# Key pages of a paged cache loaded two to a tile: one layer of a hybrid attention trunk on one core

## The chip, the cores and the metric

The kernel runs on one core of a Trainium2 chip. The core has a matrix engine (PE), whose weight loads are shown as PEld, a vector engine (DVE), an activation engine (ACT), a general engine (POOL), a queue engine (SP) and 16 DMA engines. The metric is the device time of one execution in microseconds (us). All arithmetic is float32; products that must be exact to float32 are made from a rounded high part and a low part (fp32r), so one product is three matmuls, or two where one side is used as it is.

## The reference

One layer serves a prompt of 1024 tokens and a sample group of 8 sequences with one new token each. A single input projection gives the queries, keys and values of a sparse attention (compressed blocks, selected blocks, sliding window), the input of a pooling mixer, the queries of an attention into 256 memory tokens, and gates. The three branches are gated, merged, projected and added, and a SwiGLU follows. For the sample group the past keys stand in a paged cache:

```python
past = nsa_pool_l[page_table].reshape(b, -1, 4, KV_HEADS, HEAD_DIM)
full = jnp.concatenate([past, nsa_kv], axis=1)
o_cmp, o_sel = nsa_cmp_sel(q, pos, full[:, :, 0], full[:, :, 1], full[:, :, 2], full[:, :, 3], l, w)
```

Every sequence has 16 pages of 128 tokens, 128 pages in all. Of each page the kernel needs the raw compression keys and values, summed over blocks of 32 tokens, and the scores of all selection keys against the new token's queries.

## The kernel before

All work stands in one function, `body`, and is written in stages: projections of prompt and sample together, memory attention and pooling mixer of the prompt, the sample group ("decode"), prompt attention in 32 units, merges, output projection, feed-forward. A planner at build time lists each engine's instructions in a fixed order; an engine then runs its list in that order and waits where an operand is late. The planner goes by priority, mostly the order of the program, and by when it thinks that buffers come free. Two kinds of work have low priority and fill PE's list wherever something else is late: the gate projections (`gates`, 24 tiles of 72 matmuls at L257) and the merges (`merge1f`, six tiles). A gate chunk collects in the PSUM bank `g` or `p`, one bank each, and ACT copies it out (`mg<-ps_g`, `mg<-ps_p`, L543); a bank takes the next chunk only after that copy.

SBUF tiles come from rings, in which a new tile takes a place that is free: the big ring T (12 tiles of 128x1032, `TT`), the small ring U (10 tiles of 128x512, `TU`), X (6 tiles of 128x512 for high and low parts, `TX`). T also holds what lives long in decode: the spread queries `qm` and `qmm`, the sums `pool2`, the scores `Ss`.

The stage that the change touches starts at L757. For each of 4 groups and 8 sequences, SP issues four page loads (`pages`, L724), each 128x384 into a U tile `kpg`: two times 128 columns of raw keys and values, 128 columns of selection keys. ACT rounds the selection keys to the high part `kph` (L239), POOL takes the difference `kpl` (L240), DVE sums the raw columns by blocks (L765, into `pool2`), and PE multiplies the high and low parts of the four pages with the spread queries (L768). After each group a `fold` (L729, L730) takes the scores out. Then the window keys follow (`wkt`, loaded at L778, stored again at L780, split, multiplied at L784) and the memory keys (`cmk`, loaded at L791), all in U tiles; then the selection by top-k, the value pages, and the prompt attention. In the attention, L1032 makes scores, L519 (DVE) and L522 (ACT) the softmax, L1043 to L1046 its sums, L1051 (POOL) scales, L1077 transposes, L239 and L240 split, and L1061 multiplies with the values. Merges use L1209 to L1223.

Of the kernel before, what the change touches and what calls it, by code (L numbers as in the profile page):

```python
# [10 lines left out]
ALU = mybir.AluOpType  # L11
AX = mybir.AxisListType
# [15 lines left out]
NPG = 16  # L28
# [165 lines left out]
def body(nc, tc, xT, memT, w_p, w_m, w_v, w_mk, w_mv, w_up, w_un, w_out, w_gu, w_dn, w_pool, w_cmp, gains, consts, jlt,  # L194
# [43 lines left out]
    def split(src, hi, lo, he=None, le=None):  # L238
        (he or S.copy)(hi, src)  # L239
        (le or V.tensor_sub)(lo, src, f(hi))  # L240
# [66 lines left out]
    def TU(name):  # L307
        return st_["tp"].tile([128, 512], F32, name=name, tag="U", bufs=NU)
# [101 lines left out]
    for j in range(4):  # L410
        q = proj(2 + j)
        hnorm(q, blk64, 1 / 64, gv("q"), split_sq=True)
        for s in range(2):
            h = 2 * j + s
# [301 lines left out]
    def pages(src, tab, jobs):  # L716

        p0 = jobs[0][1]
        with tc.issue_after(hist[-9].ins) if len(hist) >= 9 else nullcontext():
            rs = nc.values_load_multi_w_load_instructions(  # L720
                tab[0:1, p0:p0 + len(jobs)], engines=[mybir.EngineType.SP], min_val=0, max_val=PHYS - 1,
                skip_runtime_bounds_check_because="the table is clamped to the pages there are")[1]
        for (dst, _), r in zip(jobs, rs):
            hist.append(SY.dma_start(dst.rearrange("p (o c) -> p o c", o=1),  # L724
                                     src[bass.ds(r, 1)].rearrange("n p c -> p n c")))
# [30 lines left out]
    for g in range(4):  # L756
        ps = psum("s")  # L757
        for b in range(NB):
            h, l = TX("kph"), TX("kpl")
            kps = [TU("kpg")[:, :384] for _ in range(4)]  # L760
            pages(pgk, pts, [(kps[j], b * NPG + g * 4 + j) for j in range(4)])
            for j, kp in enumerate(kps):
                c = slice(j * 128, j * 128 + 128)
                split(kp[:, 256:], h[:, c], l[:, c], le=G.tensor_sub)
                V.tensor_reduce(pk3[:, :, b, g * 16 + j * 4:g * 16 + j * 4 + 4],  # L765
                                kp[:, :256].rearrange("p (s c l) -> p s c l", s=2, l=32), axis=AX.X, op=ALU.add)
            for x, kk in enumerate((h, l)):
                PE.matmul(ps, lhsT=qm[:, b * 128:b * 128 + 128], rhs=kk, start=b == 0 and x == 0,  # L768
                          stop=b == 7 and x == 1)
        fold(ps, Ss[(g // 2) * 64:(g // 2) * 64 + 64, (g % 2) * 512:(g % 2) * 512 + 512], 64, 512)  # L770
# [736 lines left out]
```

## Time and profile before

| | us |
|---|---|
| median of three runs | 1864.68 (1863.04 to 1869.71) |
| the profiled execution | 1865.09 |
| its span | 1863.3 |
| PE busy in the span | 1791.1 |
| DVE, ACT, POOL busy | 1210.4, 871.3, 738.1 |
| page stage: first to last page cast on ACT | 331.4 to 435.9 |
| prompt attention: first and last score matmul | 601.0 to 970.3 |

The span is the part of the execution that the trace covers. A busy time counts the instructions of an engine, not its waits; matmuls are pipelined, so the pace of a row of matmuls is read from their starts. An idle time is put down to the instruction that ended it.

### The profile page before, as it was taken

How to read it: one execution, taken by the hardware profiler on the slowest of the kernel's cores; microseconds unless marked ns; L12 is line 12 of the kernel's file. 1: busy time of each engine (PE TensorE's matmuls, PEld its weight loads, DVE VectorE, ACT ScalarE, POOL GpSimd, SP SyncE). 2: the span in 40 equal slices, each digit the busy share in tenths (PEclk: the TensorE clock that was granted, in tenths of full speed). 3: DMA queues.
4: the chain of work that ended last, by engine and by line, in shares of the span. 5: the costliest groups of instructions: out<-in, count | busy, mean ns of one | idle time of the engine just before them, and what ended most of it. 6: DMA issues, size and time to landing. Idle time of an engine off the chain costs nothing.

```text
span 1863.3 us, 34498 instructions
## 1 busy us (share of the span) xinstructions
PE 1791.1 (96%) x12337; PEld 1726.2 (93%) x12337; DVE 1210.4 (65%) x2748; ACT 871.3 (47%) x2012; POOL 738.1 (40%) x865
## 2 busy tenths in 40 slices
PE   6999999989999999989998999999999999999999
PEld 6998998888988999989998898999999999999999
DVE  8875788653555766788886835867666666635332
ACT  5743766444454766677764545423332332314100
POOL 5300211556342545467763337555455555100000
PEclk9999999899999999999999999999999999999999
DMA  4244124899665111452326643122222222546222
GB/s 169 100 142 141 63 101 164 303 303 317 202 211 169 52 47 63 140 193 90 94 84 195 196 135 95 65 85 80 70 84 80 80 86 77 170 126 183 59 68 94
DMA packets 142366, 241.13 MB, mean 129 GB/s; under 512 B 21449, under 2 KB 100450, under 8 KB 142194
## 3 DMA queue, kind: packets, MB, share of 16 engines
q1 hardware_dynamic: 118722, 189.69, 31.7%
q0 software_dynamic: 8496, 30.23, 5.0%
q10 hardware_dynamic: 14976, 19.01, 2.9%
q8 instruction: 97, 1.59, 0.4%
q14 instruction: 75, 0.61, 0.1%
HBM read 176.31 MB, written 62.55 MB: 128 GB/s over the span
## 4 chain that ended last, share of the span: by engine, by line
PE 53%; DMA 5%; DVE 4%; issue 2%; ACT 1%; POOL 1%; SPq 0%; DVEq 0%; POOLq 0%; ACTq 0%
PE ps_s L1391 10%; PE ps_t L1391 10%; PE ps_t L257 9%; PE ps_g L257 7%; PE ps_s L257 6%; PE ps_p L1061 3%; PE ps_s L1032 3%; PE ps_t L1077 2%; DMA mg<-acd 2%; PE ps_g L1391 2%; PE ps_p L1391 2%; DMA mg<-gd 1%; DMA olr<-od 1%; DMA x1d<-x 1%; DMA ad<-mg 1%
## 5 line engine op out<-in xcount | busy, mean ns | idle before, releaser
L257 PE MATMUL ps_g<-xh,wh 128*128 128x344 f32 x624 | 205.1, 329 | 4.3 <-ACT mg L543 3.9
L257 PE MATMUL ps_g<-xl,wh 128*128 128x344 f32 x624 | 201.4, 323 | 0.0
L257 PE MATMUL ps_g<-xh,wl 128*128 128x344 f32 x624 | 201.0, 322 | 0.0
L239 ACT CAST wh<-wr 128x512 fp32r<-128x512 f32 (+3 forms) x138 | 99.8, 746 | 185.4 <-PE ps_t L257 83.3
L1051 POOL TENSOR_SCALAR P<-P,st,gate 128x384 f32<-128x384 f32 (+2 forms) x192 | 127.9, 675 | 82.2 <-DVE st L1046 32.8
L239 ACT CAST cw<-tS 128x512 fp32r<-128x512 f32 x88 | 54.2, 619 | 183.9 <-PE ps_t L1391 99.4
L240 DVE TENSOR_TENSOR wl<-wr,wh 128x512 fp32r<-128x512 f32 (+3 forms) x112 | 103.7, 934 | 49.3 <-ACT wh L239 47.9
L257 PEld LDWEIGHTS ps_g<-xh,wh 128*128 128x128 f32 x624 | 118.1, 189 | 8.8 <-ACT mg L543 5.7
L522 ACT ACTIVATE P<-P,st 128x384 f32<-128x384 f32 (+2 forms) x192 | 112.2, 586 | 23.2 <-DVE st L519 21.2
L257 PEld LDWEIGHTS ps_g<-xl,wh 128*128 128x128 f32 x624 | 118.3, 190 | 1.6 <-issue 0.4
L257 PEld LDWEIGHTS ps_g<-xh,wl 128*128 128x128 f32 x624 | 118.0, 189 | 1.0 <-issue 0.2
L240 DVE TENSOR_TENSOR ptl<-ps_t,pth 128x512 fp32r<-128x512 f32 (+1 forms) x208 | 107.9, 529 | 15.6 <-ACT pth L239 14.1
L239 ACT CAST pth<-ps_t 128x512 fp32r<-128x512 f32 (+1 forms) x208 | 92.1, 457 | 52.9 <-PE ps_t L1077 37.4
L240 DVE TENSOR_TENSOR cw<-tS,cw 128x512 fp32r<-128x512 f32 x88 | 92.4, 1051 | 33.4 <-ACT cw L239 27.8
L1391 PE MATMUL ps_t<-t,cw 128*128 128x258 f32 x792 | 106.5, 283 | 2.4 <-DVE t L240 2.4
L1391 PE MATMUL ps_s<-t,cw 128*128 128x258 f32 x792 | 105.6, 282 | 2.7 <-ACT rq L274 2.7
L1391 PE MATMUL ps_s<-b,cw 128*128 128x258 f32 x792 | 107.4, 285 | 0.3 <-ACT p L1406 0.3
L1391 PE MATMUL ps_t<-b,cw 128*128 128x258 f32 x792 | 105.6, 282 | 0.3 <-issue 0.3
L1391 PEld LDWEIGHTS ps_s<-t,cw 128*128 128x128 f32 x792 | 99.5, 189 | 2.9 <-ACT rq L274 2.9
L1391 PEld LDWEIGHTS ps_t<-t,cw 128*128 128x128 f32 x792 | 99.4, 189 | 3.0 <-DVE t L240 3.0
L1391 PEld LDWEIGHTS ps_s<-b,cw 128*128 128x128 f32 x792 | 100.9, 191 | 0.7 <-ACT p L1406 0.5
L1391 PEld LDWEIGHTS ps_t<-b,cw 128*128 128x128 f32 x792 | 99.2, 188 | 0.7 <-issue 0.6
(527 smaller groups left out, 5642.0 us busy)
## 6 DMA issues: line engine op xcount, KB each, us to landing
kpg<-pg_k SPq DMA_DIRECT2D x128, 192.0 KB, 4.3
wr<-w_gu SPq DMA_DIRECT2D x44, 512.0 KB, 3.5
gd<-mg ACTq DMA_DIRECT2D x72, 172.0 KB, 3.4
wr<-w_m POOLq DMA_DIRECT2D x24, 512.0 KB, 5.5
acd<-zu SPq DMA_DIRECT2D x44, 258.0 KB, 2.1
mg<-acd SPq DMA_DIRECT2D x66, 172.0 KB, 3.2
mg<-gd SPq DMA_DIRECT2D x48, 172.0 KB, 2.4
wr<-w_p SPq DMA_DIRECT2D x16, 512.0 KB, 3.2
```

The costliest lines, as they stand in the source:

```text
L239: (he or S.copy)(hi, src)
L240: (le or V.tensor_sub)(lo, src, f(hi))
L257: PE.matmul(ps, lhsT=x, rhs=y, start=i == 0, stop=i == n - 1)
L522: S.activation(P[u], P[u], AF.Exp, bias=nm, scale=-1.0, accum_out=st[:, 6 + u:7 + u])
L1032: PE.matmul(ps, lhsT=u["q"][:, i * 128:i * 128 + 128], rhs=kk[:, k0 * 128 + a:k0 * 128 + a + n], start=x == 0, stop=x == 1)
L1051: lastp[:] = [G.tensor_scalar(p_, p_, st4[:, j, 5:6], gate[:, q, c:c + 1], op0=ALU.mult, op1=ALU.mult)]
L1061: PE.matmul(pv[:, c0:c0 + n], lhsT=lh, rhs=rhs, start=pvs["n"] == 0, stop=last, skip_group_check=True)
L1077: PE.transpose(pt_[:, x * 128:x * 128 + 128], pd[y][:, o - offs[y]:o - offs[y] + 128], ident)
L1391: PE.matmul(ps[c], lhsT=a[:, x * 512 + k * 128:x * 512 + k * 128 + 128], rhs=b[k][:, y * HT + c * HC:y * HT + c * HC + HC], start=first an ...
```

## The change

Two pages share one tile of the big ring, and the tiles of the small ring are no longer used for pages. Each page is still loaded by a DMA of its own. One ACT cast and one POOL difference round the selection keys of both pages (128x256 instead of 128x128), and the sums by blocks are made by two DVE instructions for two pages, one for keys and one for values, instead of one for each page. All lines behind it move down by three.

```diff
-            kps = [TU("kpg")[:, :384] for _ in range(4)]
-            pages(pgk, pts, [(kps[j], b * NPG + g * 4 + j) for j in range(4)])
+            kps = [TT(name="kpg")[:, :768].rearrange("p (j c) -> p j c", j=2) for _ in range(2)]
+            pages(pgk, pts, [(kps[j // 2][:, j % 2, :], b * NPG + g * 4 + j) for j in range(4)])
             for j, kp in enumerate(kps):
-                c = slice(j * 128, j * 128 + 128)
-                split(kp[:, 256:], h[:, c], l[:, c], le=G.tensor_sub)
-                V.tensor_reduce(pk3[:, :, b, g * 16 + j * 4:g * 16 + j * 4 + 4],
-                                kp[:, :256].rearrange("p (s c l) -> p s c l", s=2, l=32), axis=AX.X, op=ALU.add)
+                two_ = lambda t: t[:, j * 256:j * 256 + 256].rearrange("p (j c) -> p j c", j=2)
+                split(kp[:, :, 256:], two_(h), two_(l), le=G.tensor_sub)
+                for s in range(2):
+                    o = g * 16 + j * 8
+                    V.tensor_reduce(pk3[:, s, b, o:o + 8].rearrange("p (j c) -> p j c", j=2),
+                                    kp[:, :, s * 128:s * 128 + 128].rearrange("p j (c l) -> p j c l", l=32),
+                                    axis=AX.X, op=ALU.add)
```

Since the planner works with free places, the lists of all engines change from the page stage to the end of the merges. On SP, at the end of the page loads, the list before has the window loads (`wkt`), their stores (`o_wk`) and the memory loads (`cmk`):

```order
L724 DMA kpg<-pg_k 128x384
L778 DMA wkt<-win_k 128x512 x7
L780 DMA o_wk<-wkt 128x512
L778 DMA wkt<-win_k 128x512
L780 DMA o_wk<-wkt 128x512
L791 DMA cmk<-cm_k 128x512 x2
L780 DMA o_wk<-wkt 128x512 x5
```

On SP after the 32nd of 128 page loads, the list now has most of the same loads and the first stores:

```order
L724 DMA kpg<-pg_k 128x384
L783 DMA o_wk<-wkt 128x512
L781 DMA wkt<-win_k 128x512 x7
L794 DMA cmk<-cm_k 128x512 x2
L783 DMA o_wk<-wkt 128x512 x2
L720 TENSOR_LOAD pts
L724 ISA
L724 DMA kpg<-pg_k 128x384
```

The window transfers moved ahead of the last 96 page loads (the other stores ahead of the last 74).

On ACT, in the middle of the page stage, gate copies (`mg`, L543) and casts of gate weights (`wh`) stand between page casts; the list before:

```order
L239 CAST kph<-kpg 128x128 x6
L543 COPY mg<-ps_g 128x344
L544 DMA gd_95<-mg 128x344
L239 CAST kph<-kpg 128x128 x2
L729 COPY fold<-ps_s 64x512
L239 CAST kph<-kpg 128x128 x8
L239 CAST wh<-wr 128x512 x2
L543 COPY mg<-ps_p 128x344
```

On ACT at a like place, the list after:

```order
L239 CAST kph<-kpg 128x256 x2
L543 COPY mg<-ps_g 128x344
L544 DMA gd_95<-mg 128x344
L239 CAST kph<-kpg 128x256 x4
L239 CAST wh<-wr 128x512 x2
L543 COPY mg<-ps_p 128x344
```

Between the two gate copies stand 10 pages in 10 casts before, and 8 pages in 4 casts after.

On PE, in the last three attention units, gate and merge matmuls (L257) fill the list before:

```order
L1032 MATMUL ps_s<-kll,qst 128x256
L1061 MATMUL ps_p<-ptl,vst 128x256
L1077 MATMUL ps_t<-ct,P 128x128 x5
L1061 MATMUL ps_p<-pth,vst 128x256
L1061 MATMUL ps_p<-ptl,vst 128x256
L257 MATMUL ps_g<-xh,wh 128x344
L257 MATMUL ps_g<-xl,wh 128x344
L257 MATMUL ps_g<-xh,wl 128x344
```

On PE at the same score matmul (now L1035, values L1064, transposes L1080) the list after, out of 110 attention matmuls in a row with no L257 among them:

```order
L1035 MATMUL ps_s<-kll,qst 128x256
L1064 MATMUL ps_p<-ptl,vst 128x256
L1064 MATMUL ps_p<-pth,vst 128x256
L1080 MATMUL ps_t<-ct,P 128x128 x2
L1064 MATMUL ps_p<-ptl,vst 128x256
L1064 MATMUL ps_p<-pth,vst 128x256
L1080 MATMUL ps_t<-ct,P 128x128 x3
L1064 MATMUL ps_p<-ptl,vst 128x256
```

The L257 matmuls that stood here are now further ahead: 2676 instead of 2590 stand before the first score matmul, and as many as before (3612) before the last one.

## Rows read from the trace of the kernel before

**Rows 1.** busy times: engine, busy us (share of the span), instructions.

```profile
PE 1791.1 (96%) x12337; PEld 1726.2 (93%) x12337; DVE 1210.4 (65%) x2748; ACT 871.3 (47%) x2012; POOL 738.1 (40%) x865
```

**Rows 2.** PE, PEld, DVE, ACT, POOL busy us by stretch; clock, DMA share, GB/s.

```profile
320.00:340.00 20.00, 15.16 (x61) 11.49 (x60) 16.66 (x37) 8.05 (x19) 7.75 (x16) 0.74 0.78 261
340.00:440.00 100.00, 89.69 (x505) 83.69 (x504) 58.08 (x139) 48.88 (x155) 57.94 (x126) 0.97 0.95 312
440.00:460.00 20.00, 19.85 (x117) 18.13 (x116) 4.23 (x9) 8.91 (x17) 14.55 (x12) 1.00 1.01 375
```

**Rows 3.** groups, 340 to 440 us: busy us, mean ns | idle before, releasers.

```profile
L240 POOL TENSOR_TENSOR kpl<-kpg,kph 128x128 fp32r<-128x128 f32 x119 | 53.5, 467 | 40.2 <-ACT kph L239 38.6 <-PE ps_p L257 0.3
L765 DVE TENSOR_REDUCE pool<-kpg 128x8 f32<-128x256 f32 x119 | 48.5, 417 | 40.1 <-DMA kpg<-pg_k 36.8
L239 ACT CAST kph<-kpg 128x128 fp32r<-128x128 f32 x119 | 33.4, 300 | 49.1 <-DMA kpg<-pg_k 44.1 <-POOL kpl L240 2.0 <-PE ps_s L768 1.8
L257 PE MATMUL ps_g<-xh,wh 128*128 128x344 f32 x77 | 25.7, 333 | 3.2 <-ACT mg L543 3.2
...
L257 PE MATMUL ps_p<-xh,wh 128*128 128x344 f32 x72 | 24.1, 334 | 4.9 <-ACT mg L543 4.9
```

**Rows 4.** ACT, then PE, in order of time: start, us, instruction, idle before it.

```profile
428.97 0.30 ACT L239 CAST kph<-kpg 128x128 fp32r<-128x128 f32 x1 [2.05 <-DMA kpg<-pg_k]
...
430.22 0.43 ACT L543 COPY mg<-ps_p 128x344 f32<-128x344 f32 x1
...
430.70 0.43 PE L257 MATMUL ps_p<-xh,wh 128*128 128x344 f32 x1 [3.00 <-ACT mg L543]
```

**Rows 5.** groups, window tiles of 512 columns, 315 to 445 us.

```profile
L240 POOL TENSOR_TENSOR wkl<-wkt,wkh 128x512 fp32r<-128x512 f32 x4 | 5.2, 1288 | 4.0 <-PE ps_s L768 1.8 <-ACT wkh L239 1.5 <-PE ps_t L784 0.7
...
L239 ACT CAST wkh<-wkt 128x512 fp32r<-128x512 f32 x5 | 3.1, 620 | 3.4 <-DVE wkt L779 1.2 <-PE ps_t L784 1.1 <-PE ps_s L768 1.1
```

**Rows 6.** what SP's queue waited for, 340 to 440 us: us, times, longest.

```profile
SPq L724 <- POOL kpl L240: 12.1, 40, 0.8
```

**Rows 7.** DMA issues, 337 to 437 us: count, size, us to landing.

```profile
kpg<-pg_k SPq DMA_DIRECT2D x117, 192.0 KB, 4.3
gd<-mg ACTq DMA_DIRECT2D x18, 172.0 KB, 5.1
wr<-w_m POOLq DMA_DIRECT2D x6, 512.0 KB, 7.1
wkt<-win_k SPq DMA_DIRECT2D x7, 256.0 KB, 6.2
```

**Rows 8.** PE in order of time, in the page stage.

```profile
347.24 0.39 PE L768 MATMUL ps_s<-kph,qm 128*128 128x512 f32 x1
347.47 0.40 PE L768 MATMUL ps_s<-kpl,qm 128*128 128x512 f32 x1
...
349.33 0.32 PE L257 MATMUL ps_g<-xh,wh 128*128 128x344 f32 x1
...
353.12 0.32 PE L257 MATMUL ps_p<-xh,wh 128*128 128x344 f32 x1
```

**Rows 9.** stretch 930 to 980 us: all; L257 alone; L1214, L1222 alone.

```profile
930.00:980.00 50.00, 49.94 (x330) 47.49 (x329) 40.81 (x122) 32.79 (x92) 30.36 (x48) 1.00 0.31 91
...
930.00:980.00 50.00, 28.77 (x156) 24.56 (x155) 1.00 0.31 91
...
930.00:980.00 50.00, 6.05 (x12) 1.00 0.31 91
...
930.00:980.00 50.00, 3.29 (x6) 1.00 0.31 91
```

**Rows 10.** DVE groups, 930 to 980 us.

```profile
L240 DVE TENSOR_TENSOR wl<-wr,wh 128x512 fp32r<-128x512 f32 x4 | 2.6, 682 | 0.0
```

**Rows 11.** what PE waited for, 790 to 830 us: us, times, longest.

```profile
PE ps_t L1176 <- POOL c_s L1171: 2.9, 1, 2.9
PE ps_p L1061 <- DVE st L1043: 1.3, 1, 1.3
```
## The prediction

> **What bounds the kernel now.** I read the page's busy times first. PE is busy 1791.1 of 1863.3 us [rows 1], and the change leaves every matmul as it is (12,247 rows on PE in both builds, of the same forms), so the only time that can move is the 72 us in which PE stands idle, and the stretches that run below the full clock. [...]
>
> [...] One case in full [rows 4]: a page cast at 428.97 came 2.05 us late from its DMA, the gate copies behind it in ACT's queue ran at 430.22, and PE's next chunk began at 430.70 after 3.00 us idle. So the chain is DMA, ACT's queue, PSUM bank, PE: the page stage is limited by transfers, and gate matmuls hide what they can.
>
> **The casts and differences.** 128 ACT casts of 128x128 at 300 ns [rows 3] become 64 of 128x256. Between 300 ns for 128 columns and 620 ns for 512 [rows 5] a straight line gives 407 ns: 38.4 us become 26.0, 12.4 us less. POOL's differences go from 128 x 467 ns to 64 x 742 ns on the line to 1288 ns [rows 3, 5]: 59.8 to 47.5 us. DVE keeps 128 reductions of 256 elements at 417 ns; I take the new form at the same price, since elements and results per instruction are equal. All of this lies beside waiting: ACT was busy 48.88 of 100 us and POOL 57.94 [rows 2], and each sat about 40 us before these very instructions. I take 0 for it. Bounds: the gain is at most the 13.3 us of idle and clock that the stage has; the loss is priced as a rival.
>
> On this the row shows an ACT that waits, not one that is short of time. [...]
>
> **The ring.** Before, ten tiles of one page; the order of waits after shows eight different big tiles before the first is taken again, so 16 pages. SP waited 12.1 us in 40 pieces for a POOL difference to free a page tile [rows 6], and the DMA share was 0.95 in the stage and 0.78 in 320 to 340 [rows 2]. A deeper ring can win at most 0.05 x 100 + 0.22 x 20 = 9.4 us of transfer time, at least 0. I take 4, nearer the lower end: the DMA engines are nearly full already, and the start of the stage still waits for the last tiles of the prompt part.
>
> **What the planner moved.** With the page tiles out of the small ring, the window loads find room early: SP's order now holds all 8 window loads, their 8 stores and 2 memory loads among the pages, ahead of the last 74. These 18 transfers of 256 KB [rows 7] are 4.7 MB, at the 375 GB/s of their old place [rows 2] 12.6 us. In exchange the planner puts 549 gate matmuls between the first and last page matmul instead of 458: 91 more, 1.26 gate tiles of 72, which bring another 1.3 MB (one 512 KB load and three 172 KB stores each [rows 7]), 4.2 us at 312 GB/s. So the stage has 16.8 us more to transfer. PE's cover grows by 91 x 0.158 us (24 gate matmuls from 349.33 to 353.12 [rows 8]) = 14.4 us, plus some 13 window matmuls at 0.23 us (347.24 to 347.47 [rows 8]) = 3.0 us: 17.4. Difference: 0.6 us in favour, which I count as 0 (bounds: -2 and +4, the latter if the moved 4.7 MB run at 312 GB/s). Behind SP's stores, which wait for a DVE copy, stand page loads; the seven window and two memory loads issued ahead of them keep the DMA engines busy for 2.4 MB / 375 = 6.3 us meanwhile. The page stage as a whole: -4 us.
>
> **What is late next.** Gate and merge matmuls are the filler of the attention part too, and their number is fixed. 86 more of them stand before the first attention matmul (2676 against 2590), and the lead remains until it is paid at two places where PE's order now has none. First, between the last gate and the first merge: 76 matmuls in a row without filler against 42. Second, the end of attention: 110 in a row, where before no run reached 35.
>
> What such a run costs: in 930 to 980 us PE was full with 330 matmuls, 156 of them filler [rows 9]. 156 x 0.158 = 24.6 us, so the 174 others took 25.4 us, 0.146 each. DVE was busy 40.81 us, of it 6.05 and 3.29 for merges [rows 9] and 2.6 for weights [rows 10]; 28.9 us belong to attention, 0.166 for each of the 174. So 110 in a row need 16.0 us of PE and 18.3 us of DVE: 2.2 us idle if DVE were never late. The only row without filler is nearer to the truth: around 800 us PE waited 1.3 us for a row-sum step of DVE (L1043) and 2.9 us for POOL [rows 11] in a run of which 26 were attention matmuls; 1.3 / 26 x 110 = 5.5 us. The upper end: the tail lasts as long as before, with the 84 filler matmuls that stood there (84 x 0.158 = 13.3 us) as idle time. I take 6 for the tail and 2 for the other run (34 more, 34 x 0.05 = 1.7).
>
> **Sum.** Profiled execution 1865.1 us (span 1863.3, 1.8 around it; 0.4 above the median of the runs): -4 + 6 + 2 = +4, so **1869 us**, 0.2% slower than the median. About 0.5%, 9.3 us, is what a measurement of this kernel can tell from no change: between 1855.4 and 1874.0 counts as the same.
>
> **Rivals.** (a) The tail is not squeezed at all: one attention block waits for the next through PSUM, ACT, DVE and POOL, and the period stays. Place: PE's order behind the last merge filler; price 13.3 instead of 6: 1865.1 - 4 + 13.3 + 2 = 1876.4, slower. It decides from a tail idle of about 11 us. For it: the blocks form a chain; against it: DVE was idle 9 of 50 us there [rows 9]. Chance 0.15.
>
> (b) The pair's wait. A cast now needs two pages, so a gate copy behind it waits for one more page, 100 us / 119 pages = 0.84 us [rows 3], at the eight or so places where PE stalls: up to 6.7 us, with the ring's gain gone: 1865.1 + 6.7 + 8 = 1879.8, slower. For it: the stall at 430.70 is just this chain [rows 4]; against it: the deeper ring lets pages lie ready. It decides if PE's waits for L543 grow beyond 8.1 us [rows 3]. [...] Chance 0.12.
>
> (c) The page stage loses all its idle time, because ring and lighter ACT keep gate copies on time: -13.3 instead of -4: 1865.1 - 13.3 + 8 = 1859.8, the same by the bound; faster only if the tail costs nothing too (1852 to 1854). For it: stalls fall together with dips of the DMA share; against it: transfers per PE time are unchanged. Chance 0.20.
>
> (d) Nothing of the ring arrives, as DMA was full: 1865.1 + 8 = 1873. Chance 0.10. That the change does not do what it says is excluded by the order: 64 casts of 128x256 stand there.
>
> **How the numbers follow.** The forecast has 0.43. Faster: a third of (c) and a little of the rest, 0.08. Slower: most of (a) and (b), part of (d) and of the forecast's upper bounds, 0.24. Same: 0.68. The range reaches from just under (c), 1858, to just under (b), 1879, with about 0.1 left out on each side.
>
> **What would show it.** Right: PE idle between 340 and the last page matmul (some 17 us later than before) at 6 to 10 us; ACT still waiting for pages; the DMA share there at 0.97 or more; the first attention matmul some 10 us later; PE busy 70 to 80% in the last 20 us of attention. Wrong: page-stage waits for L543 above 8.1 us (b), none at all (c), or a full PE in the tail, which takes the 6 us away.

## The result and the profile after

The changed kernel takes 1881.34 us (median of 7 runs, 1876.57 to 1891.73) against 1867.53 us (median of 7, 1863.04 to 1871.26) for the kernel before on the same chip: a ratio of 1.0087, 95% interval 1.0070 to 1.0104. It is slower by 14 us. The forecast was 1869 us and "the same"; the upper end of the range, 1879, lies 2 us too low. The profiled execution took 1884.48 us with a span of 1882.4, 3 us above its own median, so differences of its trace to that of before (1865.09) add up to 19 us, not 14. One slow execution, 5782 us in `kv1_first` below, stands in that kernel's median (1877.05 without it) and not in its ratio.

The page stage came out nearly as it was. First the busy times by stretch (all engines, then granted clock, DMA share, GB/s), to be read beside [rows 2]:

```profile
340.00:440.00 100.00, 88.16 (x508) 82.36 (x507) 46.41 (x124) 33.57 (x84) 40.22 (x57) 0.98 0.94 316
340.00:458.20 118.20, 105.50 (x607) 98.29 (x606) 55.22 (x147) 41.59 (x102) 51.61 (x70) 0.99 0.92 305
780.00:800.00 20.00, 17.67 (x108) 15.82 (x107) 14.50 (x42) 13.80 (x36) 6.75 (x11) 0.91 1.03 321
800.00:820.00 20.00, 12.14 (x74) 11.10 (x74) 19.55 (x37) 12.85 (x30) 14.01 (x20) 0.84 0.27 87
968.00:988.00 20.00, 17.37 (x95) 12.76 (x95) 18.34 (x62) 15.13 (x45) 10.26 (x18) 1.00 0.13 41
```

Between 340 and 440 us PE has 11.8 us idle (10.3 before) and the DMA share is 0.94 (0.95); up to its last page matmul, at 458.2 us, it has 12.7 us idle at a share of 0.92. The groups of that stage show the new forms (columns as in [rows 3]):

```profile
L240 POOL TENSOR_TENSOR kpl<-kpg,kph 128x256 fp32r<-128x256 f32 x51 | 37.1, 745 | 52.7 <-ACT kph L239 37.5 <-DMA kpg<-pg_k 9.0 <-DMA gd<-mg 4.5
L767 DVE TENSOR_REDUCE pool<-kpg 128x8 f32<-128x256 f32 x102 | 36.7, 413 | 38.8 <-DMA kpg<-pg_k 38.8
L239 ACT CAST kph<-kpg 128x256 fp32r<-128x256 f32 x51 | 19.0, 406 | 45.3 <-DMA kpg<-pg_k 38.2 <-DMA o_wk<-wkt 6.7 <-ACT kph L239 0.2
```

The three prices of the prediction hold: 406 ns for a cast (407 expected), 745 for a difference (742), 413 for a reduction (417), and DVE and ACT still sit 38 us each waiting for page transfers. What PE waited for, 340 to 460 us (us, times, longest):

```profile
PE ps_s L771 <- ACT kph L239: 6.9, 4, 2.8
PE ps_g L257 <- ACT mg L543: 2.9, 3, 1.1
PE ps_p L257 <- ACT mg L543: 2.5, 3, 1.5
```

The gate banks (L543) are waited for less, 5.4 us instead of 8.1 [rows 3], the page casts more. The page casts in the kernel before, in the same window:

```profile
PE ps_s L768 <- ACT kph L239: 1.8, 3, 0.9
```

And SP's queue, 340 to 440 us, in the change and then one row of before:

```profile
SPq L724 <- DMA kpg<-pg_k: 12.0, 11, 2.8
...
SPq L724 <- POOL kpl L240: 2.5, 7, 0.6
```

```profile
SPq L724 <- DMA kpg<-pg_k: 8.4, 11, 1.3
```

The deeper ring did its work, 2.5 us of waiting for POOL instead of 12.1 [rows 6], but SP's waits for its own earlier page transfers grew from 8.4 to 12.0 us. The new loss begins at 780 to 820 us, far from the changed lines. The same stretches of the kernel before:

```profile
780.00:800.00 20.00, 20.00 (x143) 19.21 (x142) 16.40 (x47) 14.45 (x36) 6.78 (x14) 1.00 1.05 324
800.00:820.00 20.00, 14.82 (x85) 12.77 (x84) 15.79 (x55) 13.49 (x38) 16.22 (x22) 0.91 0.62 205
```

### The profile page after: what moved, and what is told of

It reads as the page before. It is cut to its first block, busy times and chain, and to the rows that moved or that the text cites. A ratio compares the mean times of both kernels' runs of the same rounds, so it can differ in the third digit from the quotient of the medians.

```text
span 1882.4 us, 34378 instructions
## 1 busy us (share of the span) xinstructions
PE 1800.3 (96%) x12337; PEld 1728.2 (92%) x12337; DVE 1215.4 (65%) x2748; ACT 860.2 (46%) x1948; POOL 728.3 (39%) x801
## 4 chain that ended last, share of the span: by engine, by line
PE 72%; DMA 9%; DVE 9%; ACT 4%; issue 4%; POOL 1%; SPq 1%; ACTq 0%; POOLq 0%; DVEq 0%
PE ps_t L257 15%; PE ps_g L257 12%; PE ps_s L1394 10%; PE ps_t L1394 9%; PE ps_s L257 7%; PE ps_p L257 4%; PE ps_p L1064 3%; PE ps_s L1035 3%; PE ps_t L1080 2%; DMA kpg<-pg_k 2%; PE ps_g L1394 2%; PE ps_p L1394 2%; DMA mg<-acd 1%; PE ps_t L932 1%; DMA gt<-gd 1%
## 5 line engine op out<-in xcount | busy, mean ns | idle before, releaser
L257 PE MATMUL ps_g<-xh,wh 128*128 128x344 f32 x624 | 204.4, 328 | 6.4 <-ACT mg L543 4.7
L257 PE MATMUL ps_g<-xl,wh 128*128 128x344 f32 x624 | 200.9, 322 | 0.0
L257 PE MATMUL ps_g<-xh,wl 128*128 128x344 f32 x624 | 200.4, 321 | 0.0
L257 PEld LDWEIGHTS ps_g<-xh,wh 128*128 128x128 f32 x624 | 117.7, 189 | 12.0 <-ACT mg L543 7.1
L257 PEld LDWEIGHTS ps_g<-xl,wh 128*128 128x128 f32 x624 | 117.9, 189 | 2.1
L240 DVE TENSOR_TENSOR ptl<-ps_t,pth 128x512 fp32r<-128x512 f32 (+1 forms) x208 | 108.0, 529 | 18.3 <-ACT pth L239 16.9
L257 PEld LDWEIGHTS ps_g<-xh,wl 128*128 128x128 f32 x624 | 117.8, 189 | 0.7
```

What stands on the lines that cost most here:

```text
L257: PE.matmul(ps, lhsT=x, rhs=y, start=i == 0, stop=i == n - 1)
```

## How the loss is placed: time less work

Equal clock times show different work in two kernels whose filler stands elsewhere. So each matmul of a trace was matched to its place in PE's order, and the work ahead of it (every matmul at the spacing that equal widths keep without a wait in the traces: 0.158 us for 344 columns as in [rows 8], 0.172 for 384, 0.229 for 512, 0.117 for 256; the medians in the trace of before are 0.158, 0.177, 0.233 and 0.118; the 0.063 taken for 128 was the author's choice and is shown by no trace: transposes start 0.109 us apart in a row and 0.028 ahead of another matmul, but their number in a stretch is nearly the same in all kernels) was taken from its start. The rest is time lost: idle, half clock (a granted 0.50, as from 814 to 820 us in the change), slow pace. The table gives, in us, what each stretch loses. "180" is the 180th of the 384 score matmuls; the handover from the first to the second KV group lies between 180 and 260. "Tail" is from the 340th score matmul to the last, "behind" from there to the feed-forward. Two profiles of the changed kernel differ by up to 1.4 us in a stretch; kernels with equal orders differ by up to 5 at the handover and by up to 7 before the last page, so a single number says less than a group of them.

| kernel | to last page | to first score | to 180 | handover | to 340 | tail | behind | rest |
|---|---|---|---|---|---|---|---|---|
| before | 62.8 | 16.5 | 14.6 | 15.8 | 6.4 | 3.7 | 17.7 | 23.0 |
| change | 63.8 | 13.2 | 16.7 | 26.6 | 8.0 | 10.0 | 17.5 | 23.9 |
| change_again | 62.4 | 13.8 | 16.6 | 25.9 | 7.9 | 9.7 | 18.2 | 23.2 |
| window_held | 63.6 | 16.6 | 17.9 | 15.9 | 5.8 | 5.9 | 10.8 | 22.5 |
| window_in_big_ring | 63.5 | 16.2 | 16.5 | 25.2 | 8.1 | 10.2 | 14.1 | 25.3 |
| ring_alone | 71.1 | 21.1 | 16.2 | 25.9 | 8.9 | 9.7 | 15.8 | 24.6 |
| ring_alone_held | 67.2 | 17.0 | 17.8 | 18.2 | 8.2 | 9.0 | 10.9 | 23.9 |
| kv1_first | 68.2 | 15.0 | 16.7 | 21.2 | 7.8 | 9.5 | 10.3 | 23.4 |
| queue_order_alone | 64.5 | 16.1 | 14.9 | 25.7 | 7.6 | 11.4 | 15.8 | 24.7 |
| queries_first | 63.9 | 15.0 | 16.2 | 23.0 | 5.1 | 7.7 | 13.4 | 24.5 |
| key_parts_from_psum | 64.1 | 16.9 | 16.6 | 23.1 | 7.2 | 9.5 | 14.2 | 22.9 |
| key_parts_from_psum_before | 65.8 | 14.9 | 15.0 | 17.3 | 7.9 | 3.7 | 16.0 | 26.0 |
| merge_moved_after | 65.5 | 15.2 | 16.6 | 23.9 | 6.7 | 6.2 | 22.3 | 24.5 |
| merge_moved_before | 69.0 | 17.0 | 15.0 | 18.7 | 5.5 | 4.0 | 16.4 | 22.7 |
| window_held_merge_moved | 60.8 | 17.4 | 17.7 | 18.2 | 5.4 | 3.9 | 16.4 | 24.1 |
| window_held_later_end | 58.6 | 16.6 | 16.1 | 20.5 | 9.4 | 4.6 | 15.1 | 23.6 |
| tail_emptied_before | 62.4 | 15.2 | 15.4 | 17.7 | 7.6 | 8.3 | 14.0 | 23.0 |

The change against before: page stage and decode -2.3, up to score 180 +2.1, handover +10.8, to 340 +1.6, tail +6.3, the rest +0.7. Against all four kernels with the order of before (15.8 to 18.7 at the handover) the +10.8 is +7.9 to +10.8; the -2.3 lies inside their spread.

## What happens at the handover

At the handover SP has two kinds of loads to issue: the queries (`qz`), values (`vz`) and keys (`kz`) of the second group, and 48 reloads of merged parts (`xh<-oh`, `xl<-ol`) into tiles that come free as the last gate tile is multiplied. SP's loads in the change and then before (count, ns, first and last start):

```profile
L1122 SPq DMA_DIRECT2D qz<-qd x2: 320/320/320, 766.3 to 782.9; - x2
...
L1111 SPq DMA_DIRECT2D kz<-kd x1: 481/481/481, 800.9 to 800.9; - x1
...
L1236 SPq DMA_DIRECT2D xl<-ol x24: 319/422/652, 763.6 to 797.9; - x24
```

```profile
L1119 SPq DMA_DIRECT2D qz<-qd x2: 319/320/320, 755.3 to 767.5; - x2
...
L1108 SPq DMA_DIRECT2D kz<-kd x1: 450/450/450, 787.5 to 787.5; - x1
...
L1233 SPq DMA_DIRECT2D xl<-ol x24: 319/382/507, 776.1 to 805.9; - x24
```

With 86 more gate matmuls ahead of the attention the gates end earlier (their last matmul runs at 784.6 us instead of 799.0), the reloads start at 763.6 instead of 776.1, and SP's list has the second group's loads behind them: both queries stand behind 3 and 27 reloads, the keys behind all 48. Before, the queries stood ahead of all reloads and the keys behind 18. By the clock the keys are issued 13.4 us later. But PE itself is 11.3 us later there (the 180th score matmul starts at 782.4 instead of 771.1): counted from that matmul, the keys are issued 2.2 us later than before, and in a second profile of the change 0.6 us. More has changed in PE's list: between the 180th and the 200th score matmul it has 19 gate and merge matmuls instead of 56, which is 37 x 0.158 = 5.8 us less to do before it needs the keys (an estimate from [rows 8]). And the keys meet the first merge. What PE waited for, 770 to 840 us in the change, to be read beside [rows 11]:

```profile
PE ps_s L1035 <- DVE kll L1116: 6.1, 1, 6.1
```

The 6.1 us are for the low parts of the keys. That subtraction, twice the same operation (min, median, max in ns), in the change and before:

```profile
L1116 DVE TENSOR_TENSOR kll<-kz,khh x2: 1220/4528/7835, 808.0 to 815.9; 64x1024 fp32r<-64x1024 f32 x2
```

```profile
L1113 DVE TENSOR_TENSOR kll<-kz,khh x2: 1216/1217/1218, 794.1 to 795.3; 64x1024 fp32r<-64x1024 f32 x2
```

One of the two took 7.84 us instead of 1.22; these 6.6 us more cover PE's wait of 6.1. POOL in that time, in the change (start, us, instruction):

```profile
808.12 2.67 POOL L1212 TENSOR_TENSOR mg<-mg,rstd 128x344 f32<-128x344 f32 x3
810.77 0.55 POOL L1054 TENSOR_SCALAR P<-P,st,gate 128x256 f32<-128x256 f32 x1
811.30 1.04 POOL L1164 TENSOR_TENSOR c_s<-c_s,q 128x512 f32<-128x512 f32 x1
812.30 2.48 POOL L240 TENSOR_TENSOR wl<-wr,wh 128x512 fp32r<-128x512 f32 x2
```

Seven operations without a gap until 814.8, most of them of the first merge; DVE's subtraction ends 1.1 us behind them, about its own length. DVE shows 19.55 us busy in 800 to 820, and 7.84 of them are this one subtraction. The subtraction's recorded start, 808.03, lies ahead of those of all seven POOL operations (the first at 808.12). What holds it is not shown by this trace. At the same place a subtraction of 7.8 to 8.0 us stands in `window_in_big_ring`, `ring_alone` and `change_again`, and two of 4.0 and 5.0 us in `merge_moved_after`: the other kernels that have this subtraction and both the lead and the change's order of loads. No other kernel of the table shows one above 2.3 us. In `merge_moved_after` the first of the two ended at 814.3, in the middle of a POOL operation that took 1.54 us (0.55 in the change):

```profile
813.17 1.54 POOL L1054 TENSOR_SCALAR P<-P,st,gate 128x256 f32<-128x256 f32 x1
```

So such a subtraction does not always end only when POOL's work is done.

## The experiments

**Is it the moved window loads, or the pairs?** `window_held`: the change, window loads kept behind the last page load.

```diff
-        SY.dma_start(t, wk2[:, b, :])
+        with tc.issue_after(hist[-1].ins):
+            SY.dma_start(t, wk2[:, b, :])
```

> The change, with one edit: the window loads may be issued on SP only behind the last page load, as they stood before. The page pairs and the big ring stay. Theory A (the loss comes from what the planner moved: window transfers into the page stage, hence 86 more gate matmuls ahead of attention, hence the second KV group's loads behind the 48 reloads of merged parts, and a tail without filler): the score matmuls now follow 2628 gate matmuls instead of 2676, the query loads stand ahead of the reloads again and the longest run without filler is 48 instead of 110, so the time is near the kernel before, 1862 to 1872 us. Theory B (waiting for both pages of a pair holds up the gate copies): the pairs are all there, so it stays near the change, 1877 to 1885 us.

1862.62 us (1857.36 to 1866.30), ratio 0.9983 (0.9966 to 0.9999). The whole loss is gone with pairs, big ring and wide casts all in place. The lead of gate matmuls falls from 86 to 38, the queries stand ahead of the reloads again (the keys behind 30), and 59 gate and merge matmuls stand between the 180th and the 200th score matmul.

`window_in_big_ring`: the kernel before, with the window tiles alone in the big ring.

```diff
-        t = TU("wkt")
+        t = TT(name="wkt")[:, :512]
```

> The kernel before, with one edit: the eight window tiles come from the big ring instead of the small one; pages, casts and page tiles are untouched. Window loads then find room among the page loads, and PE's order downstream is the one of the change (2676, 76, 110). Theory A: 1873 to 1886 us. Theory B: 1862 to 1872 us.

1883.60 us, ratio 1.0087 (1.0058 to 1.0116): the change's loss, with no page touched. The two runs settle this much: the loss hangs on where the planner puts the window loads, and rival (b), the pair's wait, is out.

**What are the pairs worth?** `ring_alone`: single pages in the big ring; `ring_alone_held`: the same with the window loads held as above.

```diff
-            kps = [TU("kpg")[:, :384] for _ in range(4)]
+            kps = [TT(name="kpg")[:, :384] for _ in range(4)]
```

> The kernel before, with one edit: each page gets a tile of the big ring, one page to a tile, one cast and one difference for each page as before. No pairs. In PE's order the attention looks as in the change: 2676 gate matmuls ahead of it, runs of 76 and 110 without filler, 46 of the 48 reloads ahead of the value loads of the second KV group. Theory A: as slow as the change, 1875 to 1886 us. Theory B (pairs): near the kernel before, 1862 to 1872 us.

> Single pages in tiles of the big ring (no pairs, so 8 pages lie ready instead of 16), with the window loads held behind the last page load. In the first round single pages in the big ring, not held, took 1893, 12 us more than the change; time less work done at the last page matmul was 77.9 us (70.9 for the change) and at the last value page 98.8 (84.1). If that loss is the shallow ring's own, this run loses 5 to 12 us against the held pairs (1862.6): 1868 to 1875. If it came from the window loads, which were spread among the pages there, it is within 3 us of them: 1860 to 1866.

1893.33 us, ratio 1.0135 (1.0105 to 1.0166), slower than either theory had it; held, 1875.32 us, ratio 1.0042 (1.0022 to 1.0062), just above the upper edge of what the shallow ring should cost. SP's longest waits, 340 to 460 us, in `ring_alone_held` and then in `window_held`:

```profile
SPq L724 <- POOL kpl L240: 15.4, 41, 1.2
```

```profile
SPq L724 <- DMA kpg<-pg_k: 13.5, 14, 3.2
...
SPq L724 <- POOL kpl L240: 2.4, 8, 0.5
```

With one page to a tile the big ring is shallower than the small one was, and SP waits for POOL again. In the same ring, with the window loads held in both, pairs are worth 0.6%, some 11 us. But only 4.0 of the 13.2 us by which the two profiles differ in the table are lost before the first score matmul; how the rest comes about is open. Against the small ring of ten single pages they are worth nothing that can be measured.

**Loads or filler?** `kv1_first`: the change, with all loads of the second group issued ahead of the 48 reloads.

```diff
-UA = 15
+UA = 13
...
+                            with tc.issue_after(ldq[0].ins):
+                                SY.dma_start(f(t[:, c0:c0 + w]), oparts[i][x][:, c0:c0 + w])
...
         if ui == UA:
             ast[1] = prep_a(1)
+            prep_v(ast[1], 1)
+            prep_k(ast[1], 1, 1)
```

> The change, with the loads of the second KV group (keys, queries, values) traced at unit 13 and the 48 reloads held on SP behind the last of them. The page stage and the 2676 gate matmuls ahead of attention stay; the runs without filler are 68 and 65. Theory A: the 6 us wait for the low key part near 817 us goes, and the handover between the two KV groups wins 5 to 10 us: 1870 to 1877 us. A rival (the handover is slow because filler is missing there, not because loads are late): 1879 to 1885 us.

1877.53 us, ratio 1.0059 (1.0041 to 1.0077), just outside the expected range. The handover loses 21.2 instead of 26.6. By the clock the keys were issued at 798.9, hardly earlier than in the change, as SP waits for score matmuls that free a tile of the big ring, 12.1 us at the second group's queries (12.0 in the kernel before) and 3.0 at its keys:

```profile
SPq L1124 <- PE ps_s L1035: 12.1, 1, 12.1
...
SPq L1113 <- PE ps_s L1035: 3.0, 1, 3.0
```

Counted from the 180th score matmul, though, that is 6.5 us earlier than before, the two subtractions of the keys take 1.2 us each, and the handover still loses 5.4 us more than before. What is missing there is filler: 17 gate and merge matmuls up to the 200th score matmul instead of 56.

`queue_order_alone`: the kernel before, with nothing but SP's order at the handover copied from the change.

```diff
+        with behind(kv and br, 47):
             SY.dma_start(z[:64, :TP], kd[br][kv * 64:kv * 64 + 64, :TP])
...
+            with behind(kv, (2, 26)[j]):
                 SY.dma_start(q, qd[kv * 2 + j])
...
+            with behind(kv, 45):
                 SY.dma_start(vz[:, br * 512:br * 512 + 512].rearrange("p (k d) -> p k d", k=8),
```

> The kernel before, pages and small ring untouched, with one thing copied from the change: SP's order at the handover. The second KV group's queries, values and keys are issued behind the 3rd, 27th, 46th and 48th of the 48 reloads of merged parts, as in the changed kernel; the gate lead stays 2590 matmuls. The longest runs without filler in PE's order become 37 (handover; 42 before, 76 in the change) and 65 (tail; under 35 before, 110 in the change). Theory A1 (what the handover costs is the late loads on SP): PE waits about 6 us for the keys of the second group near 800 us and runs at the half clock behind it, together 7 to 10 us, and 3 us more in the tail: 1876 to 1881. Rival A2 (what the handover costs is the missing filler of the longer run, and the order on SP is hidden): nothing at the handover, 3 us in the tail: 1868 to 1872.

1883.85 us, ratio 1.0094 (1.0062 to 1.0127): more than theory A1 gave, and as much as the whole change costs. The handover loses 25.7 (9.9 more than before; 7 to 10 expected), tail and the merges behind it 27.2 (21.4 before). Its keys and the stretch behind (busy by stretch as above):

```profile
L1112 SPq DMA_DIRECT2D kz<-kd x1: 450/450/450, 815.1 to 815.1; - x1
```

```profile
800.00:820.00 20.00, 12.35 (x69) 10.40 (x70) 11.23 (x33) 8.20 (x19) 11.51 (x14) 0.80 0.97 305
```

So loads that come late are enough for such a loss, with no filler missing. But the run copies the order and not the times. The first reload waits for a gate matmul, and all loads behind it stand with it; SP's longest wait for that, 745 to 805 us, here and then in the change:

```profile
SPq L1239 <- PE ps_g L257: 32.1, 6, 30.9
```

```profile
SPq L1236 <- PE ps_g L257: 7.9, 4, 7.1
```

The keys are issued 42.3 us behind the 180th score matmul here, 18.6 in the change and 16.4 before. So this run shows what late loads can cost, and not what the change's order cost in the change. PE waits here 5.6 us for POOL's step on `c_s`, the compressed scores that need the late queries, and not for a stretched subtraction.

`queries_first`: the change, SP's order put back (second group loaded from unit 13, reloads behind its queries).

```diff
-UA = 15
+UA = 13
...
-            SY.dma_start(q, qd[kv * 2 + j])
+            ldq[:] = [SY.dma_start(q, qd[kv * 2 + j])]
...
+                            with tc.issue_after(ldq[0].ins):
+                                SY.dma_start(f(t[:, c0:c0 + w]), oparts[i][x][:, c0:c0 + w])
```

> The changed kernel with its pages, its window loads and its lead of 86 gate matmuls, and SP's order at the handover put back to that of before: the second KV group's input is loaded from unit 13 instead of 15 and the 48 reloads stand behind its queries, so SP issues 2 query loads, 20 reloads, 2 value loads, 10 reloads, the keys, 18 reloads. The run without filler at the handover grows from 76 to 116, the one in the tail shrinks from 110 to 48. By time less work done, from score matmul 180 to 260 of 384, the kernel before loses 15.8 us at the handover and the changed one 26.6. Theory A1 (late loads): the handover's loss falls to 15 to 19 in spite of the longer run, the tail gives back 3 to 4, together 1867 to 1873. Rival A2 (missing filler): the loss stays at 25 to 30, 1877 to 1883.

1871.40 us, ratio 1.0032 (1.0014 to 1.0051). The time is that of A1, but the place is not: the handover still loses 23.0, below A2's range and far above A1's, and the gain stands behind it. What PE waited for, 770 to 840 us:

```profile
PE ps_s L1035 <- ACT khh L1116: 4.1, 1, 4.1
PE ps_t L1181 <- POOL c_s L1176: 2.9, 1, 2.9
```

SP's longest waits, 745 to 805 us:

```profile
SPq L1124 <- PE ps_s L1035: 12.1, 1, 12.1
```

Its reloads stand behind the second query, and that one waits 12.1 us for a score matmul, as it did before (12.0). By the clock its keys are issued at 800.2; counted from the 180th score matmul, at 15.8 us, slightly ahead of before. So here no load is late in PE's own time, the two subtractions of the keys take 1.2 us each, and still the handover loses 7.2 us more than before. The kernels side by side (us behind the 180th score matmul; filler are gate and merge matmuls from there to the 200th):

| kernel | filler | keys issued | low key parts done | lost at the handover |
|---|---|---|---|---|
| before | 56 | 16.4 | 25.5 | 15.8 |
| window_held | 59 | 17.8 | 26.0 | 15.9 |
| change | 19 | 18.6 | 34.7 | 26.6 |
| change_again | 19 | 17.0 | 33.0 | 25.9 |
| key_parts_from_psum (below) | 19 | 17.3 | 30.8 | 23.1 |
| queries_first | 19 | 15.8 | 25.4 | 23.0 |
| kv1_first | 17 | 9.9 | 20.6 | 21.2 |
| queue_order_alone | 92 | 42.3 | 50.8 | 25.7 |

Of the profiles in the first table, the eight with 56 or 59 filler matmuls there lose 15.8 to 20.5 us, 17.8 on the mean; the three with 17 or 19 and no long subtraction of the keys lose 21.2 to 23.1, 22.4 on the mean; the five with 19 and a long one lose 23.9 to 26.6, 25.5 on the mean. So missing filler costs some 5 us and the stretched subtraction some 3; these are differences of groups, and single kernels scatter as much. Loads that are 26 us late cost 10 us without either, but in the change they are only 0.6 to 2.2 us later.

**The stretched subtraction.** `key_parts_from_psum`: the change, with the low key parts taken from PSUM, so that DVE reads one SBUF operand; `key_parts_from_psum_before` is its control.

```diff
+        if kv and br:
+            for c in range(0, TP, 512):
+                ps = psum("t")
+                S.copy(ps[:64], z[:64, c:c + 512])
+                for o in range(2):
+                    V.tensor_sub(ll[o * 64:o * 64 + 64, c:c + 512], ps[:64], f(hh[:64, c:c + 512]))
```

> The changed kernel with one step of the handover done in another way: ACT copies the second group's full-context keys (64x1024) into two PSUM banks, and DVE takes the low parts from there in four pieces of 512 columns, instead of in two of 1024 from the landed tile. PE's run of 76 without filler and SP's order stay word for word. In the changed kernel one of these two subtractions took 7.84 us and the other 1.22; the long one ended 1.1 us behind the last of seven POOL operations that stood without a gap from 808.1 to 814.8. Theory P (that subtraction could not run while POOL worked): the four pieces take about 0.7 us each, PE's wait of 6.1 us for them shrinks below 2, time less work from score matmul 180 to 260 falls from 26.6 to 19 to 22, the whole to 1874 to 1878 (the planner's tail run grows from 110 to 133, up to 1 us against it). Rival A1 (the keys are late by their load alone): PE waits as long for the landed keys or for the operations queued behind them, 25 to 27 us at the handover, 1880 to 1883.

> Control: the same step done from PSUM in the kernel before, where the two subtractions took 1.22 us each and PE never waited for them. By theory P nothing is to be won: 1863 to 1869, the same as before; the handover's time less work stays at 16 to 20 us. If taking the low parts from PSUM is worth something by itself, this run is faster by as much as the run above is than the change.

1876.43 us, ratio 1.0069 (1.0050 to 1.0087); the control 1864.62 us, ratio 0.9995 (0.9982 to 1.0009). The four pieces are not stretched, 0.66 to 0.68 us each; what POOL did beside them is not shown. Other DVE operations are stretched: two with two SBUF operands (in the change 0.51 us at its shortest, and 0.28), and one with a single SBUF operand (0.16 in the change). And PE waits for what stands behind:

```profile
L1120 DVE TENSOR_TENSOR kll<-ps_t,khh x4: 661/680/684, 810.8 to 816.2; 64x512 fp32r<-64x512 f32 x4
```

```profile
812.19 1.07 DVE L1232 TENSOR_TENSOR mg<-mg 128x344 f32<-128x344 f32 x1
813.19 1.67 DVE L1174 TENSOR_TENSOR c_s<-c_s,ct 128x128 f32<-128x128 f32 x1
...
817.63 1.02 DVE L1176 TENSOR_SCALAR q<-q 128x16 f32<-128x16 f32 x1
```

```profile
PE ps_p L1064 <- DVE ptl L240: 4.0, 2, 3.8
```

The pieces take what theory P gave them, about 0.7 us; the handover does not: it loses 23.1, not 19 to 22, and PE waits 3.8 us for one of DVE's next splits where it waited 6.1 for the keys. The ratio's interval overlaps that of the change, so the gain of some 3 us is not proved by the times.

**The tail.** `merge_moved_after` and `merge_moved_before` (`NM = 6` to `NM = 7`): one merge tile more as filler.

> The changed kernel with 7 instead of 6 merge tiles as filler of the attention part (one number): 72 more filler matmuls, which until now ran behind it. The run of 110 without filler at the end of attention is gone from PE's order; the run of 76 at the handover and SP's order stay. The theory (the tail of attention costs about 7 of the 14 us lost): 1873 to 1876, the last score matmul about as many us later as the added filler is long (11 us) less 7. Rival (the tail costs nothing by itself, all is lost at the handover): 1880 to 1883.

> Control for the run above: the same one number in the kernel before. Its attention part has filler to its end already (no run of 35 or more), so the seventh merge tile has no gap to fill: 1864 to 1871 by the theory. If moving a merge tile into attention is worth something by itself (it stands behind it with its own waits), this run is faster too, 1857 to 1862, and the run above does not show the price of the tail.

1886.16 us, ratio 1.0105 (1.0065 to 1.0145), where 1873 to 1876 was expected; control 1865.61 us, ratio 1.0006 (0.9991 to 1.0020). The tail's loss fell from 10.0 to 6.2 us, and that behind it rose from 17.5 to 22.3. What PE waited for there in `merge_moved_after`, 1000 to 1180 us; in the change this wait is 1.5 us:

```profile
PE ps_t L257 <- ACT oh L239: 4.5, 1, 4.5
```

By this wait, for an operand of the next stage, the merge tile had covered loads where it stood; as filler it closed one gap and opened another. The control moved nothing ahead: 3612 gate and merge matmuls stand before its last score matmul, as without the edit, and 3684 in `merge_moved_after`. So what moving a tile costs by itself is not shown.

`window_held_merge_moved` (`NM = 7`) and `window_held_later_end` (`UG = (-4, 14, 30)`): the held change without its tail run of 48.

> The change with its window loads held behind the last page load (1862.6 in the first round) and 7 merge tiles as filler. Its run of 48 without filler at the end of attention goes; by the price of the tail per matmul (7 us for 110) that is 2 to 3 us: 1858 to 1862, faster than the kernel before. Rival: the seventh merge tile is worth nothing here, 1862 to 1864.

> The change with its window loads held behind the last page load (1862.6 in the first round) and the due times of the merge filler stretched from unit 29 to unit 30 (one number): the run of 48 without filler in the tail is gone, all else in PE's order stays to the 260th score matmul. The tail of the held kernel lost 6.0 us against 3.7 in the kernel before, so this is worth 2 us by the theory: 1859 to 1862, ratio 0.996 to 0.999 to the kernel before. Rival (the stretch behind attention takes it back, as it did with the seventh merge tile): 1862 to 1866.

1866.54 us, ratio 1.0003 (0.9986 to 1.0021), and 1870.61 us, ratio 1.0029 (1.0016 to 1.0043): both misses. Both tails fell, from 5.9 to 3.9 and 4.6; behind them the loss rose from 10.8 to 16.4 and 15.1, though neither has more filler ahead of its last score matmul than the held change (3612 in all three), only another spread of it. The second also loses 4.6 more at the handover, where PE's order is the same almost to its end; that is not explained.

`tail_emptied_before` (`NM = 6` to `NM = 5` in the kernel before): a tail run of 141 with the loads in time.

> The kernel before with 5 instead of 6 merge tiles as filler: everything up to the handover stays, but the end of attention gets a run of 141 matmuls without filler (under 35 before, 110 in the change), and one merge tile more runs behind it. Time less work from score matmul 340 to the feed-forward (tail and the merges behind it) was 21.4 us in the kernel before and 27.5 in the changed one. Theory T1 (a tail without filler costs some 6 us, as the prediction has it): it grows to 27 to 30, the whole to 1870 to 1874. Theory T2 (that loss came with the late loads at the handover and not with the run's length; the five kernels with late loads lost 24 to 29 there, whatever their run, the others 17 to 21): 17 to 22, and 1862 to 1867.5.

1869.21 us, ratio 1.0023 (1.0007 to 1.0040): between the theories. The tail loses 8.3 (3.7 before), tail and behind together 22.3 (21.4).

`change_again`: the changed kernel itself.

> The changed kernel once more, for a second profile beside the first: the numbers that all theories rest on must come again. 1878 to 1884; time less work from score matmul 180 to 260 at 24 to 28 us (26.6 in the first profile), from 340 to the feed-forward at 24 to 29 (27.5), and one subtraction of the key parts again longer than 4 us. If the handover shows below 21 or the subtraction 1.2 us, the first profile was a chance one, and the readings of the handover fall.

1881.57 us, ratio 1.0092 (1.0066 to 1.0119), and in its profile the same handover again:

```profile
L1116 DVE TENSOR_TENSOR kll<-kz,khh x2: 1218/4592/7965, 805.9 to 813.9; 64x1024 fp32r<-64x1024 f32 x2
```

```profile
PE ps_s L1035 <- DVE kll L1116: 6.3, 1, 6.3
```

No version beat the kernel before by more than a measurement can tell; `window_held`, at 0.9983 (0.9966 to 0.9999), is the fastest of them.

## Why the prediction was wrong, by its steps

**Casts, differences, reductions: right.** Prices as forecast, worth nothing, as in `window_held`. (The straight line gives 741 ns for a difference, not 742. The 13.3 us that bound the gain are 10.3 idle and 3 for a mean granted clock of 0.97 [rows 2]; some 6 us at a granted 0.50 cost that. Neither changes the sum.) The 64 casts at 406 ns instead of 128 at 300 [rows 3] are 12.4 us less on ACT; none of it reached the end. For the pair's wait, rival (b), one row could be read: PE's wait for page casts grew from 1.8 to 6.9 us, while that for gate copies fell by 2.7. But with single pages and moved window loads it is about as long, in `window_in_big_ring`, 340 to 460 us:

```profile
PE ps_s L768 <- ACT kph L239: 4.2, 4, 2.3
```

and 4.4 us in `window_held`, so the grouping is not shown to be its cause.

**The page stage, -4: neither shown nor excluded.** To the last page matmul +1.0, from there to the first score matmul -3.3, together -2.3 in the first profile and -3.1 in the second (62.4 + 13.8 against 62.8 + 16.5); kernels with equal orders differ by up to 7 before the last page. And the gain did not come as argued: PE idles 12.7 us up to the last page matmul instead of 6 to 10, and the DMA share is 0.92 there instead of 0.97 or more, so by its own signs rival (d) fits the page stage better. The last page matmul came 16.1 us later (442.1 to 458.2; 17 forecast) and the first score matmul 10.7 us later (601.0 to 611.7; 10 forecast).

**"What is late next", first run, +2: this step failed.** It priced 34 more matmuls without filler at 0.05 us each, from a row of 26 attention matmuls, and measured is +10.8 and +10.1 in two profiles. The place was right (the run stands behind the first 12 merge matmuls, its length is as counted), the price was not: with the second group's loads in time the missing filler costs 7.2 us in `queries_first` (74 more matmuls in a row than before) and 5.4 in `kv1_first` (26 more), 0.10 and 0.21 us for each. A second term was not in the sum at all: at that place the subtraction of the key parts met the merges' work on POOL and took 6.6 us longer. Without that 23.1 of the 26.6 us remain, and the gain is not proved by the times. SP's list had changed too, which the prediction did not look at; `queue_order_alone` shows that such an order can cost 10 us when the loads come 26 us late, but in the change they came 0.6 to 2.2 us later in PE's own time.

**The tail, +6: right in size, its cause only in part.** Measured is +6.3 and +6.0 in the tail. But PE was not 70 to 80% busy at the end; it was 87% in the 20 us before the last score matmul (17.37 of 20 us, 968 to 988), and idle time is the smaller part of the loss: in 948 to 968 it was busy throughout. A run without filler cost 4.6 us in the tail of the kernel before (`tail_emptied_before`), but only 0.9 with the stretch behind it, and filling it in the change won nothing. Tail and the merges behind it together lose 24 to 29 in the six profiles with the loads in the change's order and no other remedy, 17 to 22 in the others but `key_parts_from_psum` (23.7). So some of it came with the handover; how, stays open, and the 6 was partly luck.

**Rivals.** (b) gave 1879.8, nearest to the result, but not for its reason: waits for L543 fell to 5.4 us, and with the pairs in place `window_held` loses nothing. (a) gave 1876.4, and the tail lost 6, not 13. (c) did not happen: the stage kept 11.8 us idle. The forecast's sum was 15 us short of the profiled execution: 9 at the handover, 2 in the page stage, 4 in stretches taken at nothing.

## What to carry to other kernels

When a change alters how much filler is used up early, price the filler at the place where it will be missing, by a row of that place, and not by a mean of other rows: here 19 matmuls instead of 56 stood between PE and the next group's keys, 300 us away from the edit. Look at every queue on which something waits for the end of the filler as well, but compare when an operand comes with when its engine needs it: by the clock the keys were 13.4 us late, in PE's own time 2.2 at most. Where tiles come free in one ring a planner pulls later loads forward into them; if those loads should not take the place, hold them explicitly. And filler moved into a gap may have covered something where it stood, so price both ends.

## What the runs showed of the hardware

A DVE subtraction with two SBUF operands of 64x1024 took 7.84 us instead of 1.22 (7.97 in `change_again`); in the change POOL ran seven operations beside it without a gap, and it ended 1.1 us behind the last of them. In `merge_moved_after` the same operation ended after 4.0 us in the middle of a POOL operation, which took 1.54 us instead of 0.55. With one operand in PSUM, in `key_parts_from_psum`, pieces of 64x512 took 0.66 to 0.68 us, while a one-operand operation of DVE in SBUF took 1.02 us instead of 0.16. Such a stretch is counted as busy time of DVE: of the 19.55 us that it shows busy in 800 to 820, 6.6 are the stretch of one subtraction.
